# A 1-core trunk of four layers: when the delta-rule mixer's second inverse, its gating and its fill are traced

## The chip, the cores and the metric

The kernel runs on one core of a Trainium2 chip. A core has five engines, each with its own in-order queue: TensorE (PE in the profile, with its weight loads as PEld), VectorE (DVE), ScalarE (ACT), GpSimd (POOL) and SyncE (SP), and 16 DMA engines fed by queues that an engine's DMA instructions fill. The metric is device time of one execution in microseconds (us); a lower time is better.

## What is computed

One sequence of 512 tokens of width 1024 passes through four residual layers: a chunked spatial-gating MLP, a gated convolutional FFN, an RWKV-7 time mixer, a second FFN, and then a final norm. Each layer is preceded by an RMS norm. All of it is float32. The change touches the time mixer alone. Cut to that:

```python
def wkv7_scan(r, w, k, v, a, b):
    """S_t = S_{t-1} diag(w_t) + (S_{t-1} a_t) b_t^T + v_t k_t^T ; y_t = S_t r_t."""
    ...

def rwkv7_mixer(h, ...):
    ...
    r = xr @ w_r; k = xk @ w_k; v = xv @ w_v           # token-shifted inputs
    w = -jax.nn.softplus(-(w0 + jnp.tanh(xw @ w1) @ w2)) - 0.5
    a = jax.nn.sigmoid(a0 + (xa @ a1) @ a2)
    g = jax.nn.sigmoid(xg @ g1) @ g2
    ...                                                # 16 heads of 64
    y = wkv7_scan(r_h, decay, k_h, v_h, -kk, kk * a_h)
    ...                                                # group norm per head, bonus r.k.v
    return (y * g) @ w_o
```

## The kernel before

**Products.** A dense float32 product is done as three products of rounded halves, `wh*xh`, `wh*xl`, `wl*xh` (L284, L285, L286). The weights come in float32 by DMA on ACT's queue (L237), ACT casts the high half (L212), and DVE or POOL subtracts to get the low half (L213).

**The mixer's stages.** The 16 heads form 8 pairs and two groups of four pairs; the 512 tokens are 8 chunks of 64. `pairs()` makes each pair's decayed operands and products, among them one unit-triangular 64x64 matrix per head and chunk, which lands in `ti[g]` (L898). `invert(g)` inverts those of group g: ACT copies the 32x32 diagonal blocks together (L961; for group 1 two of the four are DVE's), DVE transposes them (L962), a recurrence of 31 steps on DVE (L970 a product, L971 a sum) inverts them all at once, DVE transposes the result twice (L976, L977), ACT puts it back (L981), and 32x32 products on PE with ACT's copies between (L991, L999, L994, L1001) fill the off-diagonal quadrant. Each quadrant of `ti` is 32 partitions by 32 blocks (4 pairs times 8 chunks) of 32 elements.

`scan(g)` then walks the 8 chunks of a group, one after the other: PE multiplies the chunk's operands with values and state (L1066 into `us`, L1070 into `e`), DVE copies `us` to `wt` (L1068), PE applies the inverse `ti[g]` (L1079), DVE and ACT copy one half each to `vu` (L1080, L1081), PE makes the next state (L1086), DVE adds it into the next chunk's `vu` (L1089), PE finishes `e` (L1091), ACT copies it out to `y` (L1094). The generator yields three times in a chunk. The operands `st`, `vu` and `cbt` of the next chunk are loaded by SP (L1026, L1028, L1031).

Every second chunk, `finish(g, b, y)` handles a block of 128 tokens: ACT squares (L1107), DVE sums (L1110), POOL takes the inverse square root (L337), DVE scales (L1113), PE transposes (L1117), DVE applies the norm's weight (L1120), and after every second block PE multiplies the gate (16 products `aux<-sg,gw`, L284 to L286 and L1133), DVE applies it (L1135), ACT and DVE split the result into halves for the projection (L1138, L1139). `gate_weights(g)` loads the gate's weights for a group on ACT's queue (L1011, L1012) and casts them (L212, L224, L225); `scan` calls it in chunk 1, held by `issue_after` behind the last DVE and ACT instruction traced so far. `project()` multiplies by `w_o`, 96 matmuls `mm` for a group; group 0's wait until all of group 0 is gated.

**What sets the order.** The program is traced by generators that are interleaved; a scheduler then fixes each engine's order at build. `weave(main, side, fill, rate, lag, side_rate)` counts for each yield of `main` `side_rate` steps of `side` and `rate` steps of `fill` as due, and traces as many. `RATES` has a row for each weave: its third row is `scan(0)` with `invert(1)` as the side and the last projections as fill; its fourth is `scan(1)` with `project()` as fill. Within `scan`, `step(late)` traces one step of the gating of an earlier block (`late`), placed behind the last instructions of PE and DVE. `scan(1)` receives as its first `late` the gating of group 0's last block.

Of the kernel before, what the change touches and what calls it, by code (L numbers as in the profile page):

```python
# [25 lines left out]
NCH = T // C  # L26
# [1 line left out]
GN_EPS = 64e-5  # L28
C1 = -0.5 * math.exp(-0.5)

RATES = ((1.9, 2), (1.9, 6, 2.2), (0.8, 2, 2), (0.7, 2), (2, 2), (0.7, 6, 2.2))
LEAD = 6
WB = 4
FIRST0, WAIT, STEPS = 1, 1, (2, 2, 2, 2, 2)
# [109 lines left out]
class Emit:  # L144
# [558 lines left out]
    def rwkv_main(self, r, ctx, gain):  # L703
        nc, tc, A = self.nc, self.tc, self.A
        V, S, G = nc.vector, nc.scalar, nc.gpsimd
# [17 lines left out]
        def bc(t, n):  # L723
            return t.unsqueeze(2).to_broadcast([t.shape[0], t.shape[1], n])
# [190 lines left out]
        def pairs():  # L915

            units = [type("Unit", (), {})() for _ in range(KT)]

            def start(p):
                if p >= KT:  # L920
                    return iter(())
                while p not in ks:
                    next(fill)
                if p % 2 == 0:
                    second_factors(p)
                return decay(p, units[p])

            yield from start(0)
            nxt = start(1)
            operands(0, units[0])  # L930
            for _ in nxt:
                yield
            for p in range(KT):
                nxt = start(p + 2)
                if p + 1 < KT:
                    operands(p + 1, units[p + 1])
                for _ in products(p, units[p]):
                    next(nxt, None)
                    yield
                done.add(p)  # L940

        def invert(g):
# [3 lines left out]
            tg = ti[g].rearrange("p i c t -> p (i c) t")  # L946
# [3 lines left out]
            def blocks(tag):  # L950
                return ip.tile([P, 32, 32], F32, tag=tag, bufs=1, name=self.uid(tag))

            x, li, tt = blocks("ix"), blocks("li"), blocks("tt")
# [3 lines left out]
            for n, (rows, cols) in enumerate(Q):  # L957
                if g == 1 and n % 2 == 0:
                    V.tensor_copy(x[rows], tg[rows, :, cols])
                else:  # L960
                    S.copy(x[rows], tg[rows, :, cols])  # L961
            V.transpose(li.rearrange("p s t -> p t s"), x.rearrange("p u t -> p t u"))  # L962
            for _ in range(WAIT):
                yield
# [71 lines left out]
        def scan(g, late=iter(())):  # L1036

            ih = [(i, hd) for i in range(4) for hd in range(2)]
            y = None
            for c in range(NCH):  # L1040
                last = c == NCH - 1
                if (g, c) not in chunks:
# [29 lines left out]
                if not last:  # L1072
                    s0 = tile_([P, 4, C], "wt", 4)
                    for hd in range(2):
                        G.tensor_tensor(s0[H[hd]], vu[H[hd], hd], bc(gc[H[hd], 4 * g:4 * g + 4, c], C), ALU.mult)
                self.step(late)
                yield
                for i, hd in ih:
                    nc.tensor.matmul(us[H[hd], 1, i, :], ti[g][H[hd], i, c, :], wt[H[hd], i, :], start=True, stop=True)  # L1079
                V.tensor_copy(vu[h0, 0], us[h0, 1])  # L1080
                S.copy(vu[h1, 1], us[h1, 1])  # L1081
                self.step(late)
                yield
                if not last:
                    for i, hd in ih:
# [6 lines left out]
                                     start=False, stop=True, skip_group_check=True)  # L1092
                for hd in range(2):
                    S.copy(y[H[c % 2], :, hd, :], e[H[hd], 0])  # L1094
                self.step(late)
                yield
                if c % 2 == 1:
                    yield from late
                    late = finish(g, c // 2, y)
# [44 lines left out]
        def project():  # L1144

            def load(g, m):
                return self.weights(A["wo"][m:m + 2, :, 512 * g:512 * g + 512].rearrange("m p c -> p m c"), lo_eng=G)

            ws = Ahead([lambda g=g, m=m: load(g, m) for g in range(2) for m in range(0, KT, 2)] + [self.prefetch])
            def back(m):  # L1150
                if m < KT:
                    nc.sync.dma_start(self.h[m], r.hd[m])

            for g in range(2):
                while g not in gated:
                    yield
                for m in range(KT):
                    if g == m == 0:
                        back(0)
                    if g == 0:  # L1160
                        back(m + 1)
                    if m % 2 == 0:
                        w = ws.take()
                    a = self.acc("mm")
                    yield from self.dense_steps(a, w, outs[g], c0=m % 2 * 512)
                    V.tensor_tensor(self.h[m], self.h[m], a, ALU.add)  # L1166
                    if g == 1:
                        self.absorb(m, gain)
# [7 lines left out]
        def until(gen, end):  # L1176
            for _ in gen:
                yield
                if end():
                    return  # L1180
# [3 lines left out]
        main = pairs()  # L1184
        self.weave(until(main, lambda: 3 in done), None, fill, *RATES[0], ktiles=STEPS[0])
        inv = invert(0)
        for _ in take(inv, FIRST0):
            pass
        self.weave(until(main, lambda: KT - 2 in done), inv, fill, *RATES[1], ktiles=STEPS[1])
        self.weave(main, inv, fill, *RATES[5], ktiles=STEPS[1])  # L1190
        for _ in inv:
# [9 lines left out]
        for _ in range(LEAD):  # L1201
            next(fill, None)
        self.weave(scan(0), inv, fill, *RATES[2], ktiles=STEPS[2])
        for _ in inv:
            pass
        for _ in fill:
            pass
        fill = project()
        self.weave(scan(1, left.pop()), None, fill, *RATES[3], ktiles=STEPS[3])
        self.weave(left.pop(), None, fill, *RATES[4], ktiles=STEPS[4])  # L1210
        for _ in fill:
# [71 lines left out]
```

## Time and profile before

| | |
|---|---|
| three runs | 1317.49, 1320.45, 1315.26 us (median 1317.49) |
| profiled execution | 1317.32 us, span 1315.5 us |
| mean granted TensorE clock | 0.978 |
| busy share of the span | PE 97%, DVE 64%, ACT 47%, POOL 11% |
| chain of work that ended last | PE 78%, DVE 9%, ACT 3%, issue 2%, DMA 2% |
| group 0's scan, chunk 3 to chunk 7 | opens at 804.85, ends at 839.19 us |
| group 1's scan, chunk 0 to last gating | 839.19 to about 912 us |

A row of the timeline reads: start, duration, engine, line, operation, out<-in, shapes, xcount, and in brackets how long the engine had been idle before it and which instruction's end released it. In the rows of a page or a table of groups the name is followed by the count, then the total and the mean. PE's busy time counts modelled ends of pipelined matmuls, so a busy PE is not necessarily one at full clock; the granted clock is a column of the table of windows, where 1.00 is full speed. Durations come from one execution.

### The profile page before, as it was taken

The numbers are of one execution on the slowest core, as the hardware profiler recorded it, in microseconds if no ns is written. First come the engines' busy times: TensorE is split into PE (matmuls) and PEld (weight loads), VectorE is DVE, ScalarE is ACT, GpSimd is POOL, SyncE is SP. The second block draws the span as 40 slices with busy tenths as digits, with TensorE's granted clock in tenths as the row PEclk, the third lists the DMA queues.
The fourth block names the chain that finished last, engine by engine and source line by source line (L and its number), as shares of the span: only waits on it lengthen the run. The fifth ranks groups of instructions, "written<-read, shape, count | busy, mean of one in ns | idle before, by whom it ended". The sixth has DMA issues, their size and how long they took to land.

```text
span 1315.5 us, 19526 instructions
## 1 busy us (share of the span) xinstructions
PE 1272.7 (97%) x7618; PEld 1031.3 (78%) x7618; DVE 848.5 (64%) x1365; ACT 623.8 (47%) x1062; POOL 142.8 (11%) x152
## 2 busy tenths in 40 slices
PE   8999999999999999999999998898999999999996
PEld 6878888888888888787777766676888888888886
DVE  5565488788874444865869785656687777772223
ACT  5444455555554333565657644333554444442221
POOL 3100200000000010310111012332300000000001
PEclk9999999999999999999979996999999999999998
DMA  7332345555556753245877786881333232333322
GB/s 259 88 113 80 106 151 170 167 168 174 166 173 211 224 150 108 79 136 157 251 220 205 225 209 147 207 221 41 96 96 97 96 96 96 97 92 91 101 89 76
DMA packets 100461, 188.55 MB, mean 143 GB/s; under 512 B 16912, under 2 KB 47760, under 8 KB 100368
## 3 DMA queue, kind: packets, MB, share of 16 engines
q10 hardware_dynamic: 36448, 109.46, 27.2%
q1 hardware_dynamic: 63920, 77.84, 20.7%
q8 instruction: 60, 0.98, 0.3%
q14 instruction: 33, 0.27, 0.1%
HBM read 146.70 MB, written 40.57 MB: 142 GB/s over the span
## 4 chain that ended last, share of the span: by engine, by line
PE 78%; DVE 9%; ACT 3%; issue 2%; DMA 2%; POOL 1%; ACTq 0%; DVEq 0%; SPq 0%; POOLq 0%
PE mm L284 8%; PE mm L285 8%; PE mm L286 8%; PE e L284 5%; PE e L286 5%; PE e L285 5%; PE us L284 5%; PE us L286 5%; PE us L285 5%; PE aux L284 5%; PE aux L286 5%; PE aux L285 5%; DVE tt L971 1%; DVE pr L970 1%; PE us L1066 1%
## 5 line engine op out<-in xcount | busy, mean ns | idle before, releaser
L212 ACT CAST wh<-w 128x512 fp32r<-128x512 f32 (+1 forms) x361 | 220.1, 612 | 398.8 <-PE mm L285 97.1
L213 DVE TENSOR_TENSOR wl<-w,wh 128x512 fp32r<-128x512 f32 x353 | 243.8, 692 | 186.9 <-ACT wh L212 182.8
L284 PE MATMUL mm<-mxh,wh 128*128 128x512 f32 x392 | 161.2, 412 | 0.6 <-DVE h L1166 0.4
L285 PE MATMUL mm<-mxl,wh 128*128 128x512 f32 x392 | 155.7, 397 | 0.6 <-DVE mxl L1139 0.6
L286 PE MATMUL mm<-mxh,wl 128*128 128x512 f32 x392 | 155.9, 398 | 0.3 <-DVE wl L213 0.3
L311 POOL TENSOR_TENSOR ss<-ss,sq 128x512 f32<-128x512 f32 x30 | 40.7, 1357 | 777.3 <-issue 594.8
L284 PEld LDWEIGHTS mm<-mxh,wh 128*128 128x128 f32 x392 | 74.8, 191 | 20.1 <-issue 3.2
L507 ACT ACTIVATE cv<-z,par 128x512 f32<-128x512 f32 x88 | 71.7, 817 | 36.0 <-DVE z L505 35.9
L286 PEld LDWEIGHTS mm<-mxh,wl 128*128 128x128 f32 x392 | 74.7, 191 | 17.3 <-DVE wl L213 0.6
L285 PEld LDWEIGHTS mm<-mxl,wh 128*128 128x128 f32 x392 | 74.8, 191 | 16.3 <-DVE mxl L1139 1.3
L284 PE MATMUL e<-mxh,wh 128*128 128x512 f32 x216 | 84.5, 391 | 0.0
L284 PE MATMUL us<-mxh,wh 128*128 128x512 f32 (+1 forms) x216 | 84.4, 391 | 0.0
L286 PE MATMUL us<-mxh,wl 128*128 128x512 f32 (+1 forms) x216 | 84.1, 389 | 0.0
L285 PE MATMUL us<-mxl,wh 128*128 128x512 f32 (+1 forms) x216 | 84.1, 389 | 0.0
L285 PE MATMUL e<-mxl,wh 128*128 128x512 f32 x216 | 84.0, 389 | 0.0
L286 PE MATMUL e<-mxh,wl 128*128 128x512 f32 x216 | 84.0, 389 | 0.0
L508 DVE SCALAR_TENSOR_TENSOR cv<-z,par,cv 128x512 f32<-128x512 f32 x88 | 66.1, 752 | 23.9 <-ACT cv L507 23.9
L284 PE MATMUL aux<-mxh,wh 128*128 128x512 f32 x208 | 81.2, 391 | 0.2 <-ACT wh L212 0.2
L286 PE MATMUL aux<-mxh,wl 128*128 128x512 f32 x208 | 81.1, 390 | 0.0
L285 PE MATMUL aux<-mxl,wh 128*128 128x512 f32 x208 | 80.9, 389 | 0.0
L509 DVE SCALAR_TENSOR_TENSOR cv<-z,par,cv 128x512 f32<-128x512 f32 x88 | 66.0, 752 | 2.9
L284 PEld LDWEIGHTS e<-mxh,wh 128*128 128x128 f32 x216 | 40.6, 188 | 8.7 <-issue 0.5
(1071 smaller groups left out, 2679.4 us busy)
## 6 DMA issues: line engine op xcount, KB each, us to landing
w<-in_wup ACTq DMA_DIRECT2D x88, 512.0 KB, 3.5
w<-in_wdn ACTq DMA_DIRECT2D x32, 512.0 KB, 3.6
st<-std SPq DMA_DIRECT2D x32, 384.0 KB, 5.8
std<-lq SPq DMA_DIRECT2D x32, 256.0 KB, 4.6
w<-in_wdn ACTq DMA_DIRECT2D x16, 384.0 KB, 3.3
w<-in_wsu ACTq DMA_DIRECT2D x8, 512.0 KB, 3.5
w<-in_wso ACTq DMA_DIRECT2D x8, 512.0 KB, 3.5
pw<-in_wk SPq DMA_DIRECT2D x16, 256.0 KB, 3.9
```

Source lines behind the costliest of these rows:

```text
L212: nc.scalar.copy(hi[r, :n], src)
L213: (lo_eng or nc.vector).tensor_tensor(lo[r, :n], src, hi[r, :n].bitcast(F32), ALU.subtract)
L284: mm(acc, wh, xh, start=first, stop=False)
L285: mm(acc, wh, xl, start=False, stop=False)
L286: mm(acc, wl, xh, start=False, stop=last)
L311: nc.gpsimd.tensor_tensor(self.ss, self.ss, self.sq, ALU.add)
L507: nc.scalar.activation(c, z[:, 2:], AF.Identity, scale=cw(2, i), bias=self.p("conv_b", l * 44 + i))
L508: nc.vector.scalar_tensor_tensor(c, z[:, 1:T + 1], cw(1, i), c, ALU.mult, ALU.add)
L509: nc.vector.scalar_tensor_tensor(c, z[:, 0:T], cw(0, i), c, ALU.mult, ALU.add)
L970: V.tensor_tensor(q, a, b, ALU.mult)
L971: V.tensor_tensor(tt[:, 0:nj, j + 1:32], tt[:, 0:nj, j + 1:32], q, ALU.add)
L1066: nc.tensor.matmul(us[H[hd], 0, i, :], ar(i, hd, 0), vu[:, hd, i, :], start=True, stop=True)
```

## The change

Four things are changed. In `RATES`, the third row's side rate goes from 2 to 1: a yield of `scan(0)` now traces one step of `invert(1)` rather than two. The fourth row's fill rate goes from 0.7 to 0.6. In `invert(0)`, the four copies of 32 partitions by 1024 elements become sixteen of 32 by 256, one for each pair and quadrant; `invert(1)` keeps its own. And `ahead()` takes the place of `step(late)`: it traces two steps of the gating instead of one in the first two chunks of `scan(1)`. The line numbers of the kernel after are 3 higher behind L960 and 8 higher behind L1042.

```diff
--- before.py
+++ after.py
@@ -28,7 +28,7 @@
 GN_EPS = 64e-5
 C1 = -0.5 * math.exp(-0.5)
 
-RATES = ((1.9, 2), (1.9, 6, 2.2), (0.8, 2, 2), (0.7, 2), (2, 2), (0.7, 6, 2.2))
+RATES = ((1.9, 2), (1.9, 6, 2.2), (0.8, 2, 1), (0.6, 2), (2, 2), (0.7, 6, 2.2))
 LEAD = 6
 WB = 4
 FIRST0, WAIT, STEPS = 1, 1, (2, 2, 2, 2, 2)
@@ -957,8 +957,11 @@
             for n, (rows, cols) in enumerate(Q):
                 if g == 1 and n % 2 == 0:
                     V.tensor_copy(x[rows], tg[rows, :, cols])
+                elif g == 1:
+                    S.copy(x[rows], tg[rows, :, cols])
                 else:
-                    S.copy(x[rows], tg[rows, :, cols])
+                    for u in range(0, 32, NCH):
+                        S.copy(x[rows, u:u + NCH], tg[rows, u:u + NCH, cols])
             V.transpose(li.rearrange("p s t -> p t s"), x.rearrange("p u t -> p t u"))
             for _ in range(WAIT):
                 yield
@@ -1037,6 +1040,11 @@
 
             ih = [(i, hd) for i in range(4) for hd in range(2)]
             y = None
+
+            def ahead():
+                for _ in range(2 if g == 1 and c < 2 else 1):
+                    self.step(late)
+
             for c in range(NCH):
                 last = c == NCH - 1
                 if (g, c) not in chunks:
@@ -1073,13 +1081,13 @@
                     s0 = tile_([P, 4, C], "wt", 4)
                     for hd in range(2):
                         G.tensor_tensor(s0[H[hd]], vu[H[hd], hd], bc(gc[H[hd], 4 * g:4 * g + 4, c], C), ALU.mult)
-                self.step(late)
+                ahead()
                 yield
                 for i, hd in ih:
                     nc.tensor.matmul(us[H[hd], 1, i, :], ti[g][H[hd], i, c, :], wt[H[hd], i, :], start=True, stop=True)
                 V.tensor_copy(vu[h0, 0], us[h0, 1])
                 S.copy(vu[h1, 1], us[h1, 1])
-                self.step(late)
+                ahead()
                 yield
                 if not last:
                     for i, hd in ih:
@@ -1092,7 +1100,7 @@
                                      start=False, stop=True, skip_group_check=True)
                 for hd in range(2):
                     S.copy(y[H[c % 2], :, hd, :], e[H[hd], 0])
-                self.step(late)
+                ahead()
                 yield
                 if c % 2 == 1:
                     yield from late
```

How it moves instructions, at three places. **PE, the end of chunk 2 and chunk 3 of group 0.** A printed row of x8 or x32 stands for as many pairs of records in the trace, one for each half of the partitions. L991 and L994 are the second inverse's products, L1066 to L1091 a chunk of the recurrence. Before:

```order
L1086 MATMUL us_7114<-vu_6976,cbt_6975 64x64 x8
...
L991 MATMUL aux_7218<-ix_7175,ti_5021 32x32 x32
L991 MATMUL aux_7253<-ix_7175,ti_5021 32x32 x32
L1066 MATMUL us_7302<-vu_7107,st_7105 64x64
...
L1066 MATMUL us_7302<-vu_7107,st_7105 64x64 x7
...
L1079 MATMUL us_7302<-wt_7312,ti_5020 64x64 x8
...
L994 MATMUL aux_7334<-li_7176,tt_7213 32x32 x32
L994 MATMUL aux_7369<-li_7176,tt_7213 32x32 x32
L1086 MATMUL us_7302<-vu_7107,cbt_7106 64x64 x8
```

After (L1074, L1087, L1094, L1125 are L1066, L1079, L1086, L1117 of before, and L994, L997 its L991, L994):

```order
L1094 MATMUL us_7102<-vu_6976,cbt_6975 64x64 x8
...
L1074 MATMUL us_7209<-vu_7095,st_7093 64x64 x7
...
L1125 MATMUL aux_7232<-cst,y_6893 128x128 x4
L1087 MATMUL us_7209<-wt_7219,ti_5020 64x64 x8
...
L1094 MATMUL us_7209<-vu_7095,cbt_7094 64x64 x8
...
L994 MATMUL aux_7463<-ix_7408,ti_5021 32x32 x32
L1094 MATMUL us_7374<-vu_7285,cbt_7284 64x64 x7
...
L994 MATMUL aux_7518<-ix_7408,ti_5021 32x32 x32
...
L997 MATMUL aux_7587<-li_7409,tt_7458 32x32 x32
L1087 MATMUL us_7562<-wt_7572,ti_5020 64x64 x8
L997 MATMUL aux_7638<-li_7409,tt_7458 32x32 x32
L1094 MATMUL us_7562<-vu_7368,cbt_7367 64x64 x8
```

Both groups of 64 products stood between the chunk's instructions, ahead of its L1066 and ahead of its L1086; they now stand in chunks 5 and 6.

**ACT, chunk 3 of group 0.** `ti_5021<-li` puts the transposed inverse back, `tt` and `ti<-aux` follow the products, `vu_7107` (before) and `vu_7095` (after) are chunk 3's. Before:

```order
L1094 COPY y_7113<-e_7115 64x4x64
L981 COPY ti_5021<-li_7176 32x32x32 x4
L999 COPY tt_7213<-aux_7218 32x512 x2
L999 COPY tt_7213<-aux_7253 32x512 x2
L1081 COPY vu_7107<-us_7302 64x256
L1001 COPY ti_5021<-aux_7334 32x16x32 x2
L1001 COPY ti_5021<-aux_7369 32x16x32 x2
```

After (L984, L1002, L1004 are L981, L999, L1001 of before):

```order
L1102 COPY y_7101<-e_7103 64x4x64
L984 COPY ti_5021<-li_7409 32x32x32 x4
L1089 COPY vu_7095<-us_7209 64x256
L1102 COPY y_7101<-e_7210 64x4x64 x2
...
L1002 COPY tt_7458<-aux_7463 32x512 x2
L1102 COPY y_7291<-e_7375 64x4x64 x2
L1002 COPY tt_7458<-aux_7518 32x512 x2
...
L1004 COPY ti_5021<-aux_7587 32x16x32 x2
L1089 COPY vu_7368<-us_7562 64x256
L1004 COPY ti_5021<-aux_7638 32x16x32 x2
```

The four copies of `ti_5021<-li` stay where they were and chunk 3's `vu` follows them directly; the copies of the products went to chunks 5 and 6. On DVE the transposes L976 and L977 stay ahead of chunk 3's L1068.

**ACT, chunks 0 and 1 of group 1.** `vu_7684` and `vu_7743` (before), `vu_7696` and `vu_7755` (after) are those of chunks 0 and 1, `w<-in_g` the gate weights' load, `w<-in_wo` the projection's. Before:

```order
L1081 COPY vu_7684<-us_7750 64x256
L1094 COPY y_7749<-e_7751 64x4x64 x2
L1011 DMA w_1459_7820<-in_g 128x512
L1012 DMA w_1459_7820<-in_g 32x512
L237 DMA w_1470_7903<-in_wo 128x2x512
L212 CAST wh_7905<-w_1470_7903 128x512
L212 CAST wh_7909<-w_1470_7903 128x512
L1081 COPY vu_7743<-us_7831 64x256
L212 CAST gwh_7827<-w_1459_7820 128x512
L224 CAST gw_7823<-w_1459_7820 32x512
L225 CAST gw_7823<-w_1459_7820 32x512
L1138 CAST mxh_7555<-rt_4362 128x256
```

After (L1089, L1102, L1146, L1014, L1015 are L1081, L1094, L1138, L1011, L1012 of before):

```order
L1089 COPY vu_7696<-us_7762 64x256
L1102 COPY y_7761<-e_7763 64x4x64 x2
L1146 CAST mxh_7422<-rt_4362 128x256
...
L1146 CAST mxh_7428<-rt_4362 128x256
L1014 DMA w_1462_7869<-in_g 128x512
L1015 DMA w_1462_7869<-in_g 32x512
L237 DMA w_1470_7905<-in_wo 128x2x512
L212 CAST gwh_7876<-w_1462_7869 128x512
L224 CAST gw_7872<-w_1462_7869 32x512
L225 CAST gw_7872<-w_1462_7869 32x512
L1089 COPY vu_7755<-us_7880 64x256
L212 CAST wh_7907<-w_1470_7905 128x512
```

The four casts of the gating (some left out here) stand ahead of the loads, the loads behind them, and the casts of the gate's weights ahead of chunk 1's L1089, with the projection's weights behind it. Of the sixteen copies of the first inverse, seven stand among the earlier pairs' work on ACT and nine where the four stood; on DVE the transpose L962 now stands ahead of L886, which it followed.

## The prediction

> **What bounds the kernel now.** I read the page first, then a table of windows over the delta-rule mixer, then PE's, DVE's and ACT's timelines at the places that the change touches, and the chain of waits there. Line numbers are those of the kernel before.
>
> ```profile
> span 1315.5 us, 19526 instructions
> ...
> PEclk9999999999999999999979996999999999999998
> ```
>
> Nearly every slice has TensorE at full clock; the two dents (7 and 6, slices of 32.9 us) lie in the mixer's scans, about 790 to 860 us. The windows there, with columns duration, busy PE, PE weight load, DVE, ACT, POOL, then granted clock, DMA share, GB/s:
>
> ```profile
> 744.96:748.40 3.44, 3.44 (x23) 1.71 (x23) 1.68 (x4) 3.18 (x4) 0.00 (x0) 0.51 0.15 36
> 799.57:803.00 3.43, 1.71 (x64) 1.71 (x66) 3.43 (x2) 0.00 (x0) 0.00 (x0) 0.50 0.90 232
> 803.00:823.44 20.44, 19.27 (x388) 17.31 (x386) 6.48 (x16) 11.62 (x19) 3.99 (x5) 0.50 0.65 150
> 850.80:857.60 6.80, 6.69 (x41) 5.38 (x42) 3.87 (x9) 3.81 (x9) 2.24 (x3) 0.50 1.03 268
> 857.60:904.90 47.30, 46.71 (x578) 34.86 (x577) 29.19 (x63) 15.63 (x35) 15.55 (x16) 1.00 0.60 153
> ```
>
> From 857.6 to 904.9 PE is busy 46.71 of 47.30 us: a delay that reaches 857.6 is carried to the end. Before it PE waits, and runs at half clock for 3.4, 23.9 and 6.8 us. How the chunks of the scans follow one another (PE, start and duration):
>
> ```profile
> 743.35 1.20 PE L991 MATMUL aux<-ix,ti 32*32 32x32 f32 x64 [1.66 <-DVE ix L976]
> ...
> 801.29 3.62 PE L991 MATMUL aux<-ix,ti 32*32 32x32 f32 x128 [4.68 <-DVE ix L976]
> 804.85 0.49 PE L1066 MATMUL us<-vu,st 128*64 128x64 f32 x4
> ...
> 813.51 1.44 PE L1086 MATMUL us<-vu,cbt 128*64 128x64 f32 x16
> ...
> 815.93 0.53 PE L1066 MATMUL us<-vu,st 128*64 128x64 f32 x4
> ...
> 822.13 0.53 PE L1066 MATMUL us<-vu,st 128*64 128x64 f32 x4
> ...
> 829.64 0.33 PE L1066 MATMUL us<-vu,st 128*64 128x64 f32 x2 [1.22 <-DVE vu L1089]
> ...
> 834.27 0.33 PE L1066 MATMUL us<-vu,st 128*64 128x64 f32 x2
> ...
> 839.19 0.34 PE L1066 MATMUL us<-vu,st 128*64 128x64 f32 x4
> ...
> 850.85 1.12 PE L1086 MATMUL us<-vu,cbt 128*64 128x64 f32 x16 [1.74 <-ACT vu L1081]
> ...
> 858.34 0.69 PE L1066 MATMUL us<-vu,st 128*64 128x64 f32 x16
> ...
> 908.40 0.74 PE L1117 MATMUL aux<-cst,y 128*128 128x128 f32 x4 [3.07 <-DVE y L1113]
> ```
>
> L1066 opens a chunk: 804.85 is chunk 3 of group 0, 839.19 chunk 0 of group 1, 858.34 its chunk 2. A chunk without fill takes 6.20 us at half clock (815.93 to 822.13) and 4.63 at full (829.64 to 834.27): a microsecond of half clock costs 1 - 4.63/6.20 = 0.25 us there.
>
> **Copies in pieces (first inverse).** ACT's timeline, a row of ACT's groups by shape (busy, mean ns), and DVE's timeline:
>
> ```profile
> 696.12 4.21 ACT L961 COPY ix<-ti 32x1024 f32<-32x1024 f32 x4
> ```
>
> ```profile
> L898 ACT COPY ti<-lq 64x256 f32<-64x256 f32 x26 | 10.5, 402 | 8.0 <-DVE lq L897 6.9 <-DMA std<-lq 0.9
> ```
>
> ```profile
> 699.07 0.69 DVE L886 TENSOR_TENSOR dg<-cst,gc 128x512 f32<-128x512 f32 x1 [0.59 <-PE us L908]
> 700.36 2.12 DVE L962 STREAM_TRANSPOSE li<-ix 128x1024 f32<-128x1024 f32 x1 [0.59 <-ACT ix L961]
> ```
>
> Four copies of 1.05 us become sixteen. Their price I take from L898, as wide per partition: 0.40 us. Seven move forward among the pairs' work (2.8 us of ACT, whose idle time hides them; uncovered they cost up to 1.2 us, three being ahead of one operand). Nine remain: 3.6 us for 4.21, so L962 starts 0.6 us earlier, and the recurrence behind it, which DVE bounds. But L886 (0.69 us), which ran in ACT's shadow, now stands behind L962, inside DVE's full stretch, and takes most of that back. I take -0.4. Bounds: -2.2, if moreover the 3.44 us at clock 0.51 after the 1.66 us wait went (half of it, 1.7); +1.5 with the 1.2 uncovered.
>
> **Second inverse's products later.** Before, PE meets L991 after chunk 2 and waits 4.68 us in order for DVE's transpose, at half clock from 799.57. In the new order chunk 3 stands ahead. DVE's timeline there, and ACT's:
>
> ```profile
> 799.34 1.90 DVE L976 STREAM_TRANSPOSE ix<-tt 128x1024 f32<-128x1024 f32 x1
> 801.11 1.93 DVE L977 STREAM_TRANSPOSE li<-tt 128x1024 f32<-128x1024 f32 x1
> ...
> 806.23 0.42 DVE L1068 COPY wt<-us 128x256 f32<-128x256 f32 x1 [3.19 <-PE us L1066]
> ```
>
> ```profile
> 803.08 4.20 ACT L981 COPY ti<-li 32x1024 f32<-32x1024 f32 x4 [3.97 <-DVE li L977]
> ```
>
> Chunk 3's L1066 now runs at once, but its copy L1068 is still behind both transposes on DVE (801.11 + 1.93 = 803.04), and its ACT copy L1081 behind the four of L981 (803.08 + 4.20 = 807.28, plus 0.37, the row of 850.43 below). So L1086 comes at about 807.75 and not at 813.51: -5.75. PE is still idle in two pieces there, so I keep the half clock. It ended at 823.44, which in the moved program is 817.7; the clock changes on a grid of 3.41 us (799.57, 803.0, ... 820.0), and I take 820.0: 2.3 x 0.25 = +0.6. The four groups of 64 small products now stand in chunks 5 and 6 at full clock, 4 x 1.20 = 4.8 us; waits such as the 1.22 and the 0.6 us ones at each chunk's copies cover half: +2.4. Sum -2.7. Bounds: -5.75 with the products all hidden; 0 if they hide nothing and the clock comes back a further step later.
>
> **Gating at double rate, second scan.** The last gating of group 0 moves from chunk 1 into chunk 0. What moves with it: the load of the gate weights is tied behind the last DVE and ACT instruction traced before it, and this is now L1139/L1138 of that gating. ACT's timeline in group 1's chunks 0 and 1, then DVE's, then two rows of the chain of waits with the load's time:
>
> ```profile
> 843.55 0.35 ACTq L1011 DMA_DIRECT2D w<-in_g  x1
> ...
> 849.26 1.14 ACT L212 CAST wh<-w 128x512 fp32r<-128x512 f32 x2 [4.97 <-DMA w<-in_wo]
> 850.43 0.37 ACT L1081 COPY vu<-us 64x256 f32<-64x256 f32 x1
> 850.82 0.62 ACT L212 CAST gwh<-w 128x512 fp32r<-128x512 f32 x1
> 851.34 0.61 ACT L224 CAST gw<-w 32x512 fp32r<-32x512 f32 x1
> ...
> 852.62 1.02 ACT L1138 CAST mxh<-rt 128x256 fp32r<-128x256 f32 x3
> ```
>
> ```profile
> 844.33 1.09 DVE L1113 TENSOR_TENSOR y<-y,gr 128x512 f32<-128x512 f32 x1 [0.45 <-POOL gr L337]
> ...
> 846.17 1.12 DVE L1120 SCALAR_TENSOR_TENSOR rt<-aux,par,rt 128x128 f32<-128x128 f32 x4 [0.29 <-PE aux L1117]
> ...
> 847.94 0.69 DVE L1135 TENSOR_TENSOR rt<-rt,aux 128x512 f32<-128x512 f32 x1 [0.32 <-PE aux L1133]
> ```
>
> ```profile
> 843.55 3.28 DMA w<-in_g
> ...
> 776.64 5.57 DMA w<-in_g
> ```
>
> Count from t0 = 839.19. L1113 cannot start before POOL's square root, t0 + 4.2 at the earliest; with L1120 (1.12), chunk 0's L1089, two L1135 (0.69) and the L1138s (0.40 each) behind it the gating ends near t0 + 9.9, and L1011 issues there instead of t0 + 4.4, with L1012 and the wo load (L237) behind it. The load took 3.28 and 5.57 us; I take the mean, 4.4: t0 + 14.3. In the new ACT order gwh and two gw casts (0.62, 0.61, 0.61) stand ahead of chunk 1's L1081, which then runs at t0 + 16.1 where it ran at t0 + 11.24. Queued behind it are now the two wo casts, which ran at 849.26, and the fill's matmuls wait for these. L1086 behind it: t0 + 16.6 for 11.66, +4.9. Behind L1086 one fill matmul fewer follows (at half clock (6.69 - 2 x 1.12) / 9 = 0.5 us each), and the L1138/L1139 that filled ACT and DVE there are done: I credit 1.0. So chunk 2 opens +3.9 late, and the dense stretch carries it. Bounds: +1.5 (the load in 3.28 us, and fills and the end's wait absorbing 1.3), +7 (5.57 us, no credit, 1.0 for PE's new wait at L1117 in chunk 0).
>
> **Fill rate 0.7 to 0.6.** All 96 matmuls of group 0's projection stand ahead of the last L1117 in both orders, 13 for 12 of them within the end's 3.07 us wait: 0. Bounds -1.7 (half of that wait) and +2 (fills short in a chunk, four at 0.5).
>
> **Sum** against the profiled execution, 1317.32 us (1.8 around its span, 0.17 under the median 1317.49): 1317.32 - 0.4 - 2.7 + 3.9 + 0 = 1318.1, forecast 1318, about no change. Some 0.5% (6.6 us) is what a measurement of this kernel tells from none.
>
> **Rivals.**
> A, the granted clock is spared (faster). All three half-clock windows begin at a PE wait that the change shortens or splits. If none comes: 1.7 at 744.96; 14.2 us before 817.7 at 0.25, 3.6; half of 6.69 less what then waits, 2.8. 1318.1 - 8.1 = 1310. Against: a wait of only 1.66 us dropped it before, and longer ones remain.
> B, ACT's queue held by the late gate weights (slower). Decides if the load takes over 5 us. SP's loads of the next chunk then share its fate (SP's queue):
>
> ```profile
> 841.09 6.20 SPq L1028 DMA_DIRECT2D vu<-vtd  x2
> ...
> 850.04 1.17 SPq L1028 DMA_DIRECT2D vu<-vtd  x2
> ```
>
> The first was issued beside that load and took 5.0 us more. So +1.2 for 5.57 and +5.0: 1324.3. For it: the 5.57; against: by then chunk 2's loads may have gone ahead.
> C, the change does not do what it says: the scheduler's wait only moves from L991 to L1068 and L1081, the products give all back, and the gating absorbs its delay in fills. 1317.
> [...]
>
> **How the numbers follow.** Forecast 0.36, A 0.22, B 0.22, C 0.10, D 0.10. The forecast's own range, from half of each bound, is 1313 to 1323. To leave out no more than 2 in 10 the range takes in most of A and B: 1309 to 1326. Below 1310.9 lie most of A and a little of the rest, 0.23; above 1324.1 most of B and the forecast's tail, 0.22; between, 0.55.
>
> **What would show it.** PE's wait at the products gone, and two in its place, released by chunk 3's L1068 and L1081; half clock from about 800 to 820; in group 1 a PE wait of 4 to 5 us at chunk 1's L1086, released by ACT's L1081 behind the in_g load; L962 about 0.5 us earlier; the last L1117 waiting some 3 us. It is wrong where that load lands within the old time, where the clock stays up after 800, or where chunk 3's L1086 is less than 4 us earlier relative to chunk 2.

## The result and the profile after

The changed kernel took a median of 1336.38 us (1328.06 to 1340.38, 4 runs) beside 1316.99 us (4 runs) of the kernel before: a ratio of 1.0133, 95% interval 1.0089 to 1.0177. By the ratio it is slower by 17.5 us, where a time of 1318 (1309 to 1326) was forecast. Timed once more with five runs beside the kernel before (the label after_again below) the ratio was 1.0103 (1.0087 to 1.0118). The two agree where their intervals overlap, at about 1.1%, and I take 14 to 18 us as what is to be explained. One run of after_again and one of only_pieces took far longer than the others (3362 and 1575 us) and are left out of the ratios. The profiled execution of after is one of its two longest, 1339.43 us; the second profile, of after_again, took 1329.88.

The page of the kernel after:

```profile
span 1337.6 us, 19549 instructions
...
PEclk9999999999999999999889898789999999999998
```

The granted clock has six dents between 635 and 903 us where it had two. Some of its windows at half clock (columns as before); before, the clock was down from 659.6 to 669.8, 683.5 to 686.9, 744.96 to 748.4, 799.57 to 823.44 and 850.8 to 857.6:

```profile
661.60:671.90 10.30, 10.30 (x56) 8.51 (x55) 4.65 (x9) 5.94 (x11) 1.09 (x2) 0.51 0.65 187
685.50:692.40 6.90, 6.55 (x40) 5.86 (x41) 3.45 (x8) 3.65 (x8) 0.11 (x1) 0.52 0.83 258
750.40:760.60 10.20, 10.20 (x114) 7.57 (x111) 2.81 (x4) 8.01 (x11) 0.00 (x0) 0.51 0.36 97
815.20:825.50 10.30, 6.77 (x96) 5.85 (x96) 3.47 (x11) 5.89 (x8) 1.23 (x2) 0.51 1.04 237
...
869.90:880.10 10.20, 8.11 (x39) 5.23 (x41) 1.88 (x4) 3.54 (x7) 3.67 (x4) 0.51 0.50 134
```

Between 600 and 940 us TensorE is at half clock for 75 us, against 51 before (the stretches of the clock's record added up); in after_again for 58. In the traces of before and after each of these stretches lasts a whole number of steps of 3.41 us, from 3.41 to 23.89.

To see where the time goes I took the same instructions in each trace and subtracted: the L1068 that opens chunks 0, 2 and 5 of the first scan, those of chunks 0 and 2 of the second, and the last L1117. Starts before are 774.24, 792.72, 823.51, 840.04, 859.07 and 908.40 us; the other rows are the differences to it.

| trace | scan 1 opens | its chunk 2 | its chunk 5 | scan 2 opens | its chunk 2 | last L1117 |
|---|---|---|---|---|---|---|
| after | +10.0 | +13.0 | +6.2 | +12.6 | +21.4 | +21.6 |
| after_again | +3.3 | +6.3 | -0.6 | +5.8 | +12.4 | +12.5 |
| only_pieces | +7.3 | +10.2 | +9.3 | +9.3 | +7.1 | +7.1 |
| pieces_held | +5.3 | +7.5 | +6.7 | +6.5 | +5.9 | +5.7 |
| only_side | +1.5 | +2.0 | -4.1 | +1.4 | +0.7 | +0.7 |
| no_products | +1.4 | +2.1 | -4.1 | -4.3 | -3.8 | -3.8 |
| only_gating | +2.8 | +3.1 | +2.7 | +2.4 | +9.0 | +9.2 |
| gating_early | -1.0 | -0.3 | -0.5 | -0.8 | +4.1 | +2.4 |
| no_pieces | +0.5 | +0.9 | -4.9 | +1.4 | +7.5 | +7.7 |

Three things stand in it. Ahead of the first scan's chunk 2 the change loses 6 to 13 us. From there to chunk 5 it gains 6.8, and gives 6.4 back by the second scan's start. From there to chunk 2 it loses 6.6 to 8.8, and keeps the loss. The rows also show what a single trace is worth: the kernels without the pieces have the same program up to the first scan, and open it anywhere from -1.0 to +2.8 us. In the rows with the pieces, too, part of the first column is chance: PE's instructions at 640 us are late by 2.7 us in after, 2.9 in only_pieces, 3.0 in pieces_held and 1.3 in after_again, though every engine's order is that of before up to 650 us.

The first scan's chunk 3, PE's waits and then its timeline, in the kernel after:

```profile
PE us L1087 <- DVE wt L1076: 4.5, 2, 4.0
...
PE aux L997 <- issue: 2.9, 1, 2.9
PE us L1094 <- ACT vu L1089: 2.0, 1, 2.0
```

```profile
815.99 1.12 PE L1087 MATMUL us<-wt,ti 64*64 64x64 f32 x16 [4.04 <-DVE wt L1076]
...
820.16 1.12 PE L1094 MATMUL us<-vu,cbt 128*64 128x64 f32 x16 [1.99 <-ACT vu L1089]
...
843.75 0.37 PE L997 MATMUL aux<-li,tt 32*32 32x32 f32 x6 [2.95 <-issue]
```

The wait of 4.68 us at the products is gone and two stand in its place, 4.04 and 1.99 us, with the releasers that the prediction named. The third row is new and was not foreseen: in the middle of a group of 64 products PE stops for 2.95 us, released by nothing that the profile shows.

The second scan, PE, then ACT, then PE at chunk 2 and at the last transposes:

```profile
851.77 0.34 PE L1074 MATMUL us<-vu,st 128*64 128x64 f32 x4
...
856.77 1.11 PE L1125 MATMUL aux<-cst,y 128*128 128x128 f32 x4 [1.20 <-DVE y L1121]
...
865.70 0.68 PE L1087 MATMUL us<-wt,ti 64*64 64x64 f32 x16 [1.32 <-DVE wt L1076]
...
868.96 0.68 PE L1094 MATMUL us<-vu,cbt 128*64 128x64 f32 x14 [1.66 <-ACT vu L1089]
871.99 0.80 PE L284 MATMUL mm<-mxh,wh 128*128 128x512 f32 x1 [2.35 <-ACT wh L212]
```

```profile
864.01 0.35 ACTq L1014 DMA_DIRECT2D w<-in_g  x1
...
866.73 0.62 ACT L212 CAST gwh<-w 128x512 fp32r<-128x512 f32 x1 [2.02 <-DMA w<-in_g]
...
868.54 0.37 ACT L1089 COPY vu<-us 64x256 f32<-64x256 f32 x1
871.32 0.62 ACT L212 CAST wh<-w 128x512 fp32r<-128x512 f32 x1 [2.41 <-DMA w<-in_wo]
```

```profile
879.65 0.79 PE L1074 MATMUL us<-vu,st 128*64 128x64 f32 x16
...
929.97 0.63 PE L1125 MATMUL aux<-cst,y 128*128 128x128 f32 x4 [3.02 <-DVE y L1121]
```

Chunk 0 opens at 851.77. The load is issued 12.2 us later (9.9 forecast), takes 2.6 (4.4 forecast), chunk 1's copy runs at +16.8 (16.1 forecast) and its L1094 at +17.2 (16.6 forecast, 11.66 before). Behind that the fill's first product waits 2.35 us for the cast of a `w_o` weight, which waits for its load. Chunk 2 opens at +27.9, where it was +19.15 before and +23.05 was forecast. The traces of after_again, only_gating and no_pieces agree up to L1094 (load at +12.2, L1094 at +17.0 to +17.3); there the fill waits only 0.5 to 1.0 us and chunk 2 opens at +25.3 to +25.8. The wait at the end is as long as it was.

### The profile page after: what moved, and what is told of

It reads as the page before. It is cut to its first block, busy times and chain, and to the rows that moved or that the text cites. A ratio compares the mean times of both kernels' runs of the same rounds, so it can differ in the third digit from the quotient of the medians.

```text
span 1337.6 us, 19549 instructions
## 1 busy us (share of the span) xinstructions
PE 1283.6 (96%) x7618; PEld 1037.2 (78%) x7618; DVE 851.1 (64%) x1365; ACT 625.9 (47%) x1074; POOL 142.4 (11%) x152
## 4 chain that ended last, share of the span: by engine, by line
PE 83%; DVE 6%; ACT 2%; issue 2%; DMA 1%; POOL 1%; ACTq 0%; DVEq 0%; SPq 0%; POOLq 0%
PE mm L284 8%; PE mm L285 8%; PE mm L286 8%; PE e L284 5%; PE e L285 5%; PE e L286 5%; PE us L284 5%; PE us L285 5%; PE us L286 5%; PE aux L284 5%; PE aux L286 5%; PE aux L285 5%; PE aux L908 1%; DVE tt L974 1%; PE e L1099 1%
```

## The experiments

Times are medians beside the kernel before on the same chip; that kernel's median was 1318.15, 1318.37, 1318.43 and 1317.88 us in the four sets.

### Each part alone

only_pieces is the first block of the diff below on the kernel before, only_side the second, only_gating the fourth row's 0.6 with the whole of `ahead()`, and no_pieces the kernel after without the first block.

```diff
+                elif g == 1:
+                    S.copy(x[rows], tg[rows, :, cols])
                 else:
-                    S.copy(x[rows], tg[rows, :, cols])
+                    for u in range(0, 32, NCH):
+                        S.copy(x[rows, u:u + NCH], tg[rows, u:u + NCH, cols])
...
-RATES = (..., (0.8, 2, 2), (0.7, 2), ...)
+RATES = (..., (0.8, 2, 1), (0.7, 2), ...)
```

> The kernel before with the first inverse's four copies cut into sixteen, nothing else. Theory 1, each part has a fixed price as read from the trace after: that trace is 10 us late when the first scan opens (784.25 against 774.24), with only the pieces acting on what is ahead, so this kernel takes about 1327 us. Theory 2, the order is worth next to nothing itself and the clock decides: TensorE is at half clock for some 24 us more in the trace after (75 us against 51 between 600 and 940 us), where waits fall on the clock's grid is chance, so the time is anywhere from 1315 to 1330, the runs of one kernel differ by 5 us or more, and the time follows the mean granted clock (0.01 of it some 13 us). By the prediction's own sum: -0.4, 1316.6.

> The kernel before with the third row's side rate 1, nothing else. Theory 1: in the trace after, chunk 3 to chunk 5 of the first scan gain 6.8 us against chunk 2 (from +13.0 to +6.2), and the products in chunks 5 to 7 give 6.4 back (to +12.6 at the second scan's start), so about -0.4: 1316.6 us. Prediction's sum: -2.7, 1314.3. Theory 2: 1312 to 1322, by the mean clock.

> The kernel before with the gating at double rate in the second scan's first two chunks and the fill rate 0.6, nothing else. Theory 1: the trace after loses 8.8 us from the second scan's chunk 0 to chunk 2 (from +12.6 to +21.4) and keeps it: about 1325.8 us. Prediction's sum: +3.9, 1320.9, at most +7. Theory 2: the delay without the clock's part is the 4.9 us of the queue; 1319 to 1326.

> The kernel after with the first inverse's four whole copies back: side rate, gating and fill rate as after. Theory 1: the parts add, -0.4 + 8.8: about 1325.4 us, and 11 us under the kernel after. Prediction's sum: +1.2, 1318. Theory 2: it doesn't follow from the parts; the sum of the single parts' differences is missed by 5 us or more.

| kernel | median us | ratio to before | 95% interval | forecast by the prediction's sum |
|---|---|---|---|---|
| only_pieces | 1325.48 | 1.0048 | 1.0035 to 1.0061 | -0.4 us |
| only_side | 1318.39 | 1.0010 | 0.9998 to 1.0022 | -2.7 us |
| only_gating | 1327.56 | 1.0067 | 1.0055 to 1.0079 | +3.9 us |
| no_pieces | 1324.44 | 1.0042 | 1.0025 to 1.0059 | +1.2 us |

The single parts add to 0.48 + 0.10 + 0.67 = 1.25%, and no_pieces with the pieces to 0.90%; the one lies within the interval of the first timing of the kernel after, the other within that of the second. They do not add closely: no_pieces, which is the side rate and the gating together, costs 0.42%, where the two alone add to 0.77%, more than the intervals allow, and why is open. But two parts have a price of their own, and the theory that the clock's luck makes the whole loss falls: the runs of only_pieces (without the one left out) and of only_gating agree with themselves to 4 us and lie clear of before. All three terms of my sum were too low, the pieces' by 6.7 us, the gating's by 5, the side rate's by 4.

### What in the pieces costs

```diff
+                    for u in range(0, 32, NCH):
+                        with tc.issue_after(self.last(mybir.EngineType.Activation)):
+                            S.copy(x[rows, u:u + NCH], tg[rows, u:u + NCH, cols])
```

> The kernel before with the first inverse's copies cut into sixteen, each tied behind ACT's last instruction so that all stay where the four stood; the order of all other work is as before. Theory 1, what costs in the pieces is the order that they bring along (seven pieces among the earlier pairs' work, and the weights' casts L738 and their subtractions L739 some 20 places earlier on ACT and 13 on DVE): then that part goes, and what is left is the pieces' own time, 16 x 0.40 = 6.4 us for 4.2, which delays DVE's transpose L962 and the recurrence by 2.2: about 1320. Rival, the pieces themselves cost the 7.3 us (more instructions, each with its fixed part): 1325 or more.

1319.53 us, ratio 1.0013 (0.9992 to 1.0035): +1.7 us where 2.2 were expected from the pieces' own time. So 4.6 of the 6.3 us of only_pieces (1.3 to 7.9 by the two intervals) go when the pieces are held: they are not the pieces' own time but come with the order that the free pieces bring. (The order is not all as before in pieces_held either: behind 700 us PE's and DVE's differ, the recurrence being later.) One change of the order is plain. In the kernel before (DVE):

```profile
678.27 0.68 DVE L897 TENSOR_TENSOR lq<-aux,cst 128x512 f32<-128x512 f32 x1
...
691.79 0.42 DVE L739 TENSOR_TENSOR l<-w,l 64x256 fp32r<-64x256 f32 x1
```

In only_pieces, DVE, then ACT, then PE's waits from 600 to 775 us:

```profile
681.53 1.45 DVE L739 TENSOR_TENSOR l<-w,l 64x256 fp32r<-64x256 f32 x1
...
683.51 0.67 DVE L897 TENSOR_TENSOR lq<-aux,cst 128x512 f32<-128x512 f32 x1
```

```profile
684.22 0.41 ACT L898 COPY ti<-lq 64x256 f32<-64x256 f32 x1 [3.04 <-DMA wl<-wvd]
...
685.23 0.63 ACT L832 ACTIVATE sq<-kn 128x512 f32<-128x512 f32 x1
```

```profile
PE e L842 <- ACT sq L832: 3.0, 2, 2.5
```

The scheduler, with ACT's work cut finer, put one cast of the next pair's weights (L738) 20 places earlier on ACT, the pieces not counted, and its subtraction (L739) 13 places earlier on DVE. The subtraction took 1.45 us there, not 0.42, ahead of L897; L898 and behind it L832 come later on ACT (the 3.04 us before L898 are put down to a DMA here and to L897 in the trace of after), and PE waits 2.5 us at L842. In the trace of after this wait is 2.7 us, in that of after_again 1.0; before, PE's waits there were two of 0.6 at most:

```profile
PE e L842 <- ACT sq L832: 1.1, 2, 0.6
```

Behind it the clock was at half speed for 6.8 us in only_pieces and in after (from 685.9 and 685.4), for 3.4 in after_again and before. What this place costs is not shown. From 672 to 694 us of before's time only_pieces and after lose 4.5 us and after_again 1.4; but pieces_held, where L739 stands as before, loses 2.8 there, with a wait of 1.27 us at L842 and 6.8 us at half clock. The rest I can place but not take apart: about 1 us from 711 to 741, and 2.9 to 3.0 from the first scan's opening to its chunk 2, in each of the three traces whose pieces are free; the kernels without pieces have 0.0 and 0.3 to 1.9.

### What in the gating costs

```diff
-                if c == 1:
+                if c == 1 - g:
                     with ExitStack() as behind:
                         ...
                         gw[g] = gate_weights(g)
```

gating_early has this edit on only_gating, early_load on the kernel before; fill_only is before with 0.6 in the fourth row.

> The kernel before with the double-rate gating and fill rate 0.6 (9.4 us slower by itself), and the second group's gate weights traced in chunk 0 and not in chunk 1, so that their load is issued some 8 us earlier, ahead of the gating's casts, and chunk 1's L1081 no longer waits for it. Theory 1, the loss is ACT's queue held by the load (load 2.6 to 5.6 us and what of its issue was late): 5 us or more come back, 1322 or less. Rival, the loss is the gating's own work put into chunk 0 (PE's wait at L1117, 16 products, DVE's L1120, L1135, L1139 ahead of the next chunk's L1068): 1326 to 1328.

> The kernel before with the second group's gate weights traced in chunk 0 and not in chunk 1, and nothing else. Theory 1, the load holds ACT's queue before the change too, for less: PE waits 1.74 us at chunk 1's L1086 there, and the chain of waits shows 3.28 us of the load; 2 to 3 us come back, 1315.5. Rival: the rest of that chunk is PE's and the fill only moves: 1318.

> The kernel before with the fill rate of the second scan 0.6 and not 0.7, nothing else. Prediction's term: 0, bounds -1.7 and +2, so 1316.7 to 1320.4. If so, all of the 9 us of the gating edit belongs to the double rate; rival, the fill's part is 3 us or more, 1321 and over.

gating_early: 1321.18 us, 1.0016 (1.0003 to 1.0030), so 6.7 of the 8.8 us are back: with the load ahead of the gating most of that loss is gone. The edit moves the fill as well (chunk 1's L1086 stands behind 15 fill products there, at 21.6 us behind chunk 0's opening, and chunk 2 opens at +23.2), so it bears out that the late load brings the loss, and does not show each step between. fill_only: 1319.63, 1.0018 (1.0001 to 1.0034), +2.4 us, a little over the bound of 2 that I had given: its profile shows 1.7 us lost at the end, between the second scan's last chunk and the last L1117, and the double rate is left with about 0.5%. The 2.1 us that stay in gating_early, which has the fill rate too, are no more than this, so the gating's own work in chunk 0 has no price that these runs show.

early_load was to gain and lost: 1328.17 us, 1.0076 (1.0062 to 1.0089). Its ACT, its PE and its chain of waits say why:

```profile
862.87 1.14 ACT L212 CAST wh<-w 128x512 fp32r<-128x512 f32 x2 [13.91 <-DMA w<-in_wo]
```

```profile
864.45 1.12 PE L1086 MATMUL us<-vu,cbt 128*64 128x64 f32 x16 [12.50 <-ACT vu L1081]
```

```profile
850.34 12.50 DMA w<-in_wo
```

With the gate's load out of the way, the scheduler put the casts of the second projection weights ahead of chunk 1's L1081. That load was issued beside SP's loads of the next chunks, took 12.50 us, and PE stood still for as long; the DMA engines were full meanwhile (the last but one number of the window):

```profile
854.00:858.00 4.00, 0.00 (x0) 0.00 (x0) 0.00 (x0) 0.00 (x0) 0.00 (x0) 0.59 1.08 212
```

It is the mechanism of the prediction's rival B, with another load, in an experiment that I had built to remove it.

### Where the gain of chunk 3 goes

> The kernel before with side rate 1, and the second inverse's off-diagonal products (L991, L994 and ACT's copies of them) left out, so that chunks 5 and 6 hold only their own work; group 1's output is not the reference's. Theory 1, what the products cost in chunks 5 to 7 (4.4 to 5.7 us in three traces) eats what chunk 3 gained: about 5 us under the kernel with side rate 1 alone, 1313. The prediction's half (2.4 us hidden in waits): 1316. Rival, the payback is not the products but the clock's drop in those chunks: 1317 or more.

```diff
             for i in range(2):
+                if g == 1:
+                    yield
+                    yield
+                    continue
                 for hf in range(2):
```

With the second inverse's products left out the kernel takes 1313.60 us, 0.9951 (0.9933 to 0.9970), by the medians 4.8 under only_side and by the ratios 7.8 (4.9 to 10.7). So the gain of chunk 3 is real (5.6 to 6.9 us from chunk 2 to chunk 5 in all traces with side rate 1), and what comes with the products takes it back. How, shows PE's timeline of only_side:

```profile
822.97 1.20 PE L991 MATMUL aux<-ix,ti 32*32 32x32 f32 x64
...
825.32 1.20 PE L991 MATMUL aux<-ix,ti 32*32 32x32 f32 x64
826.45 0.34 PE L1066 MATMUL us<-vu,st 128*64 128x64 f32 x4
...
827.58 1.20 PE L994 MATMUL aux<-li,tt 32*32 32x32 f32 x64
...
829.32 1.13 PE L994 MATMUL aux<-li,tt 32*32 32x32 f32 x59
...
833.46 0.28 PE L994 MATMUL aux<-li,tt 32*32 32x32 f32 x5 [3.00 <-issue]
...
835.47 0.52 PE L1066 MATMUL us<-vu,st 128*64 128x64 f32 x4
```

And of no_products, whose L1070 is the L1066 of before:

```profile
825.30 0.33 PE L1070 MATMUL us<-vu,st 128*64 128x64 f32 x2 [1.22 <-DVE vu L1093]
...
829.92 0.33 PE L1070 MATMUL us<-vu,st 128*64 128x64 f32 x2
```

A stop of 3.00 us stands in the last group, as in after; no_products has none. At chunk 4's end (822.7 us) the two traces agree to 0.1 us. The two groups of L991, 2.4 us, then delay chunk 5 by 1.2, the wait of 1.22 us having covered the rest. Chunk 5 takes 9.0 us where it took 4.6: 3.0 of the 4.4 more are the stop, and 1.4 are L994's two groups. Chunk 6 takes 0.2 more, in part at half clock. Together 5.9 us: the products themselves cost some 2.6 of their 4.8 us, about the half that I had, and the stop costs 3.0. Three more kernels moved the products:

> Side rate 1, and the second inverse's products traced in eight steps of 32 and not four of 64, so that a step (0.6 us) can hide in the 0.6 us waits of PE at each chunk's copies. Theory 1, products cost what they don't hide: half of the 4.8 us comes back against side rate 1 alone (1318.4), about 1316. Rival, any product between the chunk's instructions delays them by its whole length: 1318.

```diff
-                    for u in range(16):
-                        for hd in range(2):
+                    for hd in range(2):
+                        if g == 1 and hd:
+                            yield
+                        for u in range(16):
```

1333.99 us, 1.0131 (1.0110 to 1.0151). It has no such stop, but its edit raised the price of the products themselves, and the sort is not held to group 1: the first inverse's four groups, which took 1.20 to 1.29 us each before, are sorted too, and the first scan opens at +6.9 us. PE in side_split, at half clock:

```profile
847.83 1.92 PE L996 MATMUL aux<-li,tt 32*32 32x32 f32 x32 [0.20 <-ACT ti L1003]
```

Thirty-two of these records take 1.92 us, where before the 128 at half clock took 3.62 (801.29): sorted by half of the partitions they cost 60 ns each, alternating between the halves 28. (Each product of the code leaves two records. They are not one for each half of the partitions, as said above: the records of L1066 show all 128 partitions.) From chunk 7 to the second scan's opening the trace loses 6.8 us more than before, with such groups still among the chunk's instructions. So the run is no answer to the question that it was built for.

> Both of the last two edits together: products in eight steps at side rate 1, and the gate weights' load in chunk 0. If both theories hold, 1313 to 1314, 0.3% under the kernel before; if neither, 1318.

1336.08 us, 1.0140 (1.0118 to 1.0162), 0.1% above side_split, where early_load alone lost 0.76%: the losses do not add. In its trace the load's loss is there, 8.4 us from the second scan's opening to its chunk 2, but less is lost ahead of it (9.2 us against 13.9), and why is open.

> The kernel before with side rate 1.75 and not 2: of the second inverse's four product groups the first now stands behind chunk 3's L1066, the second and third behind its L1079, all ahead of its L1086, the fourth behind that. Theory 1, a product costs only where it stands in PE's order: PE is idle there for 5.1 us (waiting for L1068) and 2.0 us (L1081) in the kernel with side rate 1, so L991's two groups fill idle time and only L994's wait for ACT's copies; 2 to 4 us under side rate 1 and under the kernel before, 1314 to 1316. Rival, the third group waits in order for ACT's copies as L994 did before the change and nothing comes of it: 1318.

> The kernel before with side rate 1.6: the first group behind chunk 3's L1079, the second and third behind its L1086, the fourth ahead of chunk 4's L1079. Chunk 3's L1086 then waits for no product but the first: it keeps the 5.8 us that chunk 3 gained at side rate 1. Theory 1: three groups of 1.2 to 1.8 us between the instructions of chunks 3 and 4 cost at most 4, and PE's stop of 3.0 us in the fourth group (the same record, 9921, in four traces with side rate 1) doesn't come, since the products are not followed by chunks that run as densely: 1315 to 1317. Rival, the stop comes with the products wherever they stand: 1318.

side_175 took 1317.45 us, 0.9993 (0.9978 to 1.0008), side_16 1320.97, 1.0028 (1.0016 to 1.0040). In side_175 there is no stop, PE waits 2.9 us at L991 for DVE's transpose and 2.0 at L994 for ACT's copies, and the start of chunk 5 is 1.0 us earlier against chunk 2 than before; the rival of that run holds, nothing comes of it. In side_16 PE stops for 1.5 us in an L994 group. At none of the places tried do the products come free: by the medians only_side, side_175 and side_16 lie 3.9 to 7.4 us above no_products. No kernel tried here that has all of the products beats the one before.

### What the clock is worth

```diff
-                    ps = self.acc("aux").rearrange("p (u t) -> p u t", t=32)
+                    ps = self.acc("aux")
+                    if g == 1 and i == hf == 0:
+                        for _ in range(18):
+                            nc.tensor.matmul(ps, sg[0][:, 0:P], sg[1], start=True, stop=True)
+                    ps = ps.rearrange("p (u t) -> p u t", t=32)
```

> The kernel before with 18 products of 128x512 more (their result is overwritten and never read), in the 4.68 us in which TensorE waits for the second inverse's transpose, ahead of L991. They take 18 x 0.235 = 4.2 us and end before the transpose does. Theory 2, the wait's real price is the clock that it brings down: half clock from 799.57 to 823.44 goes; the two pairs of product groups save 2 x 1.2 us each way (7.24 to 4.8), chunks 3 to 5 save 0.25 of some 12 us: 5 to 6 us faster, about 1312. Rival, the clock drops all the same (the engines' waits in chunks 3 to 5 do it) or ACT and DVE bound those chunks: 1317 to 1319.

1318.38 us, 1.0000 (0.9984 to 1.0016). The filler did its work, and the gain went elsewhere. Windows, then PE's timeline of warm:

```profile
800.00:810.50 10.50, 6.83 (x188) 5.60 (x186) 5.43 (x7) 6.22 (x10) 0.67 (x1) 1.00 0.88 203
810.50:820.70 10.20, 9.88 (x212) 9.02 (x212) 2.66 (x8) 5.05 (x10) 1.23 (x2) 0.50 0.39 86
```

```profile
798.21 4.38 PE L987 MATMUL aux<-sg,sg 128*128 128x512 f32 x18
...
803.12 2.21 PE L995 MATMUL aux<-ix,ti 32*32 32x32 f32 x128 [0.53 <-DVE ix L976]
...
809.79 0.45 PE L1083 MATMUL us<-wt,ti 64*64 64x64 f32 x8 [2.75 <-issue]
```

The clock stays up through 800 to 810, the 128 products (L995 here) take 2.21 us and not 3.62, chunk 3's L1068 comes 1.8 us earlier against chunk 2. Then PE stops for 2.75 us without a releaser, the clock drops at 810.5, and chunk 4 is 0.3 us late. So the full clock gave 1.8 us by chunk 3, and the stop and the later drop of the clock took them: the run does not tell what the clock is worth by itself.

### The kernel after once more

> The kernel after once more, beside the kernel before on the same chip, since its first four runs lie 12 us apart. Theory 1, the parts add: pieces 0.48%, side rate 0.10%, gating with fill 0.67%, together 1.25%: about 1334. Rival, together they cost more than apart (the clock's drops meet): the 1.33% or more of the first runs, 1336 to 1340. The other way, from no_pieces (0.42%) and the pieces (0.48%): 0.90%, 1330.

1331.83 us, 1.0103 (1.0087 to 1.0118), between the two sums. That the parts together cost more than apart is not borne out.

## Why the prediction was wrong

- **Copies in pieces, -0.4 us (bounds -2.2 and +1.5): measured +0.48%, 6.3 us.** This is the step that failed, and the one term that left its bounds clearly. I priced the copies and the two or three neighbours that the new order shows near them, and put the knock-on at no more than 1.2 us. pieces_held shows that my price for the copies themselves was fair (1.7 us, and there all sixteen stand behind); 4.6 of the 6.3 us come with the new order of the pairs' work from 650 us on, for which my sum had no term. Which instructions of that order make it stays open; L739 ahead of L897 is a candidate. L962 came 4.3 us later in only_pieces, not 0.5 earlier; 2.8 of the 4.3 were there before the first piece. I also read the page wrongly here: of the two dents of the kernel before, the 7 is the slice from 657.8 to 690.6 us and lies in the pairs' work, at half clock from 659.6 to 669.8 and from 683.5 to 686.9, and not in the scans. My windows left out this stretch, in which the free pieces change the order.
- **Second inverse's products, -2.7 us: measured +0.1% (-0.3 to +2.9 us).** The first half was right in mechanism and size: the wait moves to L1068 and L1081, and chunk 3's L1086 comes 6.4 us earlier against chunk 2 in the trace after (5.75 forecast). The products' own price in chunks 5 and 6 was right too, some 2.6 us in only_side's trace for the 2.4 forecast. What the sum had at nothing is PE's stop of 3.0 us among them, and with it chunk 3's gain is given back. The half clock that I kept from 800 to 820 lasted 10.2 us, from 815.1 to 825.3, and no run prices it alone.
- **Gating at double rate, +3.9 us (bounds +1.5 and +7): measured with the fill rate +0.67%, 8.8 us (7.2 to 10.4).** The mechanism was right in its order: L1011 behind the gating's casts, gwh and gw ahead of chunk 1's L1081, L1086 at t0 + 17.2. gating_early bears it out by taking 6.7 us back. That 17.2 lies so near the 16.6 forecast is partly luck: the load was issued 2.3 us later than I had it, since I left out PE's sixteen products of the gate (3.5 us in chunk 0, at half clock, where they took 2.2 before), and it landed 1.8 us faster. What failed is the credit of 1.0 us behind L1086 and what follows there: from L1086 to chunk 2 it took 10.7 us in after and 8.3 to 8.5 in the other three traces with the double rate (7.5 before), because the wo casts now follow L1081 and the fill waits for them, in after at half clock from 869.7. At L1086 itself PE waits 1.66 us, not the 4 to 5 that I had forecast; in after there are besides it 1.20 ahead of the transposes, 1.32 at L1079 and 2.35 at the fill.
- **Fill rate, 0: measured +0.18%, 2.4 us (0.1 to 4.5),** past the bound of 2 by a little, and the bound lies within the interval. The last L1117 waits 3.02 us as forecast.

As to the rivals: A (the clock is spared) is refuted, since the half clock grew, from 51 to 75 us; it also spoke of all three half-clock windows, where the trace before has five between 600 and 905 us. B named the right mechanism for the wrong load: the gate weights took 2.6 us, under the 5 us that it needed, and the loss came all the same because they are issued so late; in early_load a `w_o` load of 12.50 us did what B had described. B's 5.0 us was misread: the row of 6.20 us spans two of SP's loads, issued at 841.09 and 846.85, and they landed after 5.09 and 3.49 us. C came true in the first scan alone, and there half of what is given back is the stop. Steady work did not bring the clock back at once in after: from 750.4 PE was busy for 10.20 us on end, with the clock at 0.51 all the while.

The range missed because all four terms missed to the same side, and because I had bounded the order's knock-on by the price of single instructions.

## What to carry to other kernels

Where a scheduler fixes the order at build, a small edit is priced by all that it moves, not by what it adds: hold its place (as pieces_held does) or leave it. Where a load is tied behind the last instruction traced, moving work ahead of that point moves the load, and every cast in the same in-order queue with it (issue at +12.2 us in after, +4.4 before). A product that is moved out of a wait into a denser chain still costs what the waits there do not cover (2.6 of 4.8 us here), and a stop that no wait of the trace before announces can take the rest of the gain (3.0 us here).

## What was not expected of the hardware

PE stops for 2.75 to 3.0 us that no semaphore explains, after dense runs of small matmuls at full clock (1.00 up to the stop in after, only_side and warm). In only_side, no_pieces, after and after_again it is at the same place, with 5 or 6 of 64 records of the last L994 group to come, though these lie up to 11 us apart in time; in after 9921 records of PE's queue, weight loads among them, are ahead of it. The trace also records 16 KB packets of a queue named "instruction" (q8 on the page), 60 in before and 60 in after, where PE's queue has 15341 and 15344 records; whose they are is not shown. In before 173 to 360 records of PE's queue lie between the starts of two packets from 781 to 841 us. In after it is 506 ahead of the stop: the packets start at 835.06 and 840.88, the stop is from 840.81 to 843.75, and PE goes on 1.5 us after the second packet ends. side_16 has a shorter stop, of 1.49 us, in an L994 group too. What PE stops for is not shown: no run changed one thing there alone. The kernel before has no such stop there; its products run at half clock, at which 128 of them take 3.62 us.

Small matmuls of 32x32 that alternate between the two halves of the partitions cost about half of those that don't: 28 and 60 ns a record at half clock (above). At full clock the alternating ones take 19 (1.20 us for 64 in before).
